# Cutting the first load of a streaming kernel into a 2 KiB head and a 62 KiB body

The kernel runs on one core of one Trainium2 chip. The metric is the device time of that core in microseconds (us), median of several executions. The record calls a kernel slower or faster only from 2% on.

## The reference

```python
x = randn(1024, 4096) float32, axis = -1
mean = np.mean(x, axis=axis, keepdims=True)
out  = ((x - mean) ** 2).astype(np.float32)
```

16.78 MB are read and 16.78 MB written; every row needs all of its 4096 columns before its mean is known.

## The kernel before

Four rows lie side by side in each partition, so 1024 rows make two tiles of 128 partitions x 64 KiB. Each tile is loaded by one DMA and stored by one, and the statistics and squares of a tile are shared between the scalar engine (ACT) and the vector engine (DVE).

```python
x_t = x.rearrange("(n p q) d -> n p (q d)", p=P, q=Q)      # Q = 4 rows a partition
tiles = []
for i in range(ntiles):                                     # ntiles = 2
    x_tile = io.tile([P, Q * D], F32)                       # 64 KiB a partition
    nc.sync.dma_start(out=x_tile, in_=x_t[i])
    tiles.append(x_tile)
# ...
for i in range(ntiles):
    row = [tiles[i][:, q * D:(q + 1) * D] for q in range(Q)]
    m3 = mean_on_act(row[3])
    m0 = mean_on_dve(row[0])
    # ... means of rows 1 and 2, squares in place on ACT and DVE
    nc.sync.dma_start(out=out_t[i], in_=tiles[i])
```

## Time and profile before

| | before |
|---|---|
| time, median of the first 3 runs | 83.25 us (83.16 to 83.27) |
| span in the profile | 81.4 us |
| DMA queue q1 | 96.0% of the span, 576 packets, 33.55 MB |
| DVE, ACT busy | 41%, 43% |

How to read it: the busy shares are of the whole span. A DMA packet here is one run of one partition, so its size is the run length, and each of the 16 DMA engines moves 8 packets of each 64 KiB transfer. After its data each transfer has one 4-byte packet an engine that bumps the semaphore. The lines that carry this are in the prediction below.

### The profile page before, as it was taken

The numbers are of one execution on the slowest core, as the hardware profiler recorded it, in microseconds if no ns is written. First come the engines' busy times: TensorE is split into PE (matmuls) and PEld (weight loads), VectorE is DVE, ScalarE is ACT, GpSimd is POOL, SyncE is SP. The second block draws the span as 40 slices with busy tenths as digits, with TensorE's granted clock in tenths as the row PEclk, the third lists the DMA queues.
The fourth block names the chain that finished last, engine by engine and source line by source line (L and its number), as shares of the span: only waits on it lengthen the run. The fifth ranks groups of instructions, "written<-read, shape, count | busy, mean of one in ns | idle before, by whom it ended". The sixth has DMA issues, their size and how long they took to land.

```text
span 81.4 us, 79 instructions
## 1 busy us (share of the span) xinstructions
DVE 33.4 (41%) x16; ACT 34.7 (43%) x13; POOL 0.2 (0%) x4
## 2 busy tenths in 40 slices
DVE  0000000000089999999439999999900000000000
ACT  6000000000089999999339999999800000000000
POOL 0000000000000000000000000000000000000000
DMA  9099956999982999992999992999997499998390
GB/s 483 32 515 515 483 258 290 515 515 515 515 386 129 515 515 515 515 451 129 451 515 515 515 483 129 418 515 515 515 515 322 193 515 515 515 515 386 161 483 0
DMA packets 577, 33.55 MB, mean 412 GB/s; under 512 B 65, under 2 KB 65, under 8 KB 65
## 3 DMA queue, kind: packets, MB, share of 16 engines
q1 hardware_dynamic: 576, 33.55, 96.0%
q14 instruction: 1, 0.00, 0.0%
HBM read 16.78 MB, written 16.78 MB: 412 GB/s over the span
## 4 chain that ended last, share of the span: by engine, by line
DMA 50%; DVE 21%; SPq 0%; issue 0%
DMA x_tile<-in_x_dram 50%; DVE neg_sum L62 16%; DVE x_tile L85 2%; DVE x_tile L84 1%; DVE neg_mean L65 1%; SPq L46 0%
## 5 line engine op out<-in xcount | busy, mean ns | idle before, releaser
L62 DVE TENSOR_REDUCE neg_sum<-x_tile 128x1 f32<-128x4096 f32 x6 | 26.5, 4413 | 25.2 <-DMA x_tile<-in_x_dram 25.2
L69 ACT ACTIVATE x_tile<-x_tile,neg_mean 128x4096 f32<-128x4096 f32 (+1 forms) x8 | 26.0, 3323 | 0.1
L54 ACT ACTIVATE copy<-x_tile 128x4096 f32<-128x4096 f32 x2 | 7.2, 3617 | 23.3 <-DMA x_tile<-in_x_dram 23.3
L85 DVE TENSOR_TENSOR x_tile<-x_tile 128x1792 f32<-128x1792 f32 x2 | 4.1, 2026 | 0.1
L84 DVE TENSOR_SCALAR x_tile<-x_tile,neg_mean 128x1792 f32<-128x1792 f32 x2 | 2.3, 1154 | 0.1
L54 ACT ACT_TABLE_LOAD x1 | 1.3, 1283 | 0.7 <-PEq L103 0.7
L65 DVE TENSOR_SCALAR neg_mean<-neg_sum 128x1 f32<-128x1 f32 x6 | 0.9, 154 | 0.2
L54 ACT ACTIVATION_READ_ACCUMULATOR copy<-x_tile 128x1 f32 x2 | 0.4, 187 | 0.0
L103 POOL MEMSET const-bfloat16-1.0<- 128x1 bf16 x1 | 0.1, 101 | 0.0
L103 POOL MEMSET const-uint8-127<- 128x1 uint8 x1 | 0.1, 101 | 0.0
L103 POOL MEMSET const-float32-0.0<- 128x1 f32 x1 | 0.1, 98 | 0.2 <-issue 0.2
L103 POOL MEMSET const-float32-1.0<- 128x1 f32 x1 | 0.1, 98 | 0.0
## 6 DMA issues: line engine op xcount, KB each, us to landing
x_tile<-in_x_dram SPq DMA_DIRECT2D x2, 31.4
out_dram<-x_tile SPq DMA_DIRECT2D x2, 21.7
```

The lines of the kernel that those rows point to most:

```text
L54: nc.scalar.activation(out=copy, in_=row, func=ACT.Identity, scale=-inv_d, accum_out=neg_mean)
L62: inorder(nc.vector.reduce_sum(out=neg_sum, in_=row, axis=mybir.AxisListType.X, negate=True))
L65: inorder(nc.vector.tensor_scalar_mul(out=neg_mean, in0=neg_sum, scalar1=inv_d))
L69: inorder(nc.scalar.activation(out=part, in_=part, func=ACT.Square, bias=neg_mean, scale=1.0))
L84: nc.vector.tensor_scalar_add(out=back, in0=back, scalar1=m2)
L85: nc.vector.tensor_mul(out=back, in0=back, in1=back)
L103: nc = _bacc.Bacc("TRN2", target_bir_lowering=False, num_devices=1)
```

## The change

Its intent: let the first transfer begin with a short one. Load 0 becomes a head of 512 columns (2 KiB a partition) and a body of the rest (62 KiB). Load 1 and both stores keep their 64 KiB runs.

```diff
+    HEAD = 512
...
-        nc.sync.dma_start(out=x_tile, in_=x_t[i])
+        cuts = [0, HEAD, Q * D] if i == 0 else [0, Q * D]
+        for lo, hi in zip(cuts, cuts[1:]):
+            nc.sync.dma_start(out=x_tile[:, lo:hi], in_=x_t[i][:, lo:hi])
```

## The prediction

> **What bounds the kernel now.** I read the page first, then the chain of waits, then the timeline, then a table of stretches cut at the four transfers, and last the records of the single DMA packets in the trace. The page's top lines:
>
> ```profile
> DVE 33.4 (41%) x16; ACT 34.7 (43%) x13; POOL 0.2 (0%) x4
> ...
> DMA  9099956999982999992999992999997499998390
> ...
> DMA packets 577, 33.55 MB, mean 412 GB/s; under 512 B 65, under 2 KB 65, under 8 KB 65
> ...
> q1 hardware_dynamic: 576, 33.55, 96.0%
> ```
>
> No compute engine is busy for half the span, while one DMA queue is busy for 96% of it. The dips in the tenths (0, 2, 3) are no idle time: a packet is booked in the slice where it starts, and a packet of 64 KiB lasts 2.4 us, longer than the 2.0 us slice. The 576 packets are 4 transfers x 128 partitions = 512 data packets of 64 KiB, and 4 x 16 = 64 semaphore packets (4 B, 9 ns each).
>
> The chain of waits alone would mislead. It gives DMA 50% and DVE 21% and stops at 58.9 us, at the last vector instruction, in front of the final store. The table of stretches (start:end, us, DVE, ACT, POOL, clock, DMA share, GB/s), cut by me at the transfers, corrects that:
>
> ```profile
> 0.00:1.70 1.70, 0.00 (x0) 0.97 (x1) 0.20 (x4) 1.00 0.00 0
> 1.70:21.60 19.90, 0.00 (x0) 0.31 (x1) 0.00 (x0) 1.00 1.01 422
> 21.60:40.98 19.38, 16.71 (x8) 16.72 (x6) 0.00 (x0) 1.00 1.00 433
> 40.98:60.40 19.42, 16.71 (x8) 16.72 (x6) 0.00 (x0) 1.00 1.00 432
> 60.40:80.30 19.90, 0.00 (x0) 0.00 (x0) 0.00 (x0) 1.00 0.97 422
> 80.30:81.40 1.10, 0.00 (x0) 0.00 (x0) 0.00 (x0) 1.00 0.00 0
> ```
>
> Load, load, store, store follow one another without a pause; the DMA share is 1.00 in the middle, and all compute (16.7 us a tile) lies beside transfers of 19.4 us. So the time is: start until packets move, 32 packets per engine in a row (4 transfers x 128 / 16), and a tail. From the timeline, the two places where the queue could run dry:
>
> ```profile
> 0.73 0.86 SPq L46 DMA_DIRECT2D x_tile<-in_x_dram  x2
> ...
> 39.68 0.35 SPq L86 DMA_DIRECT2D out_dram<-x_tile  x1
> 42.05 3.62 ACT L54 ACTIVATE copy<-x_tile 128x4096 f32<-128x4096 f32 x1 [2.59 <-DMA x_tile<-in_x_dram]
> ```
>
> The packet records give the rest, in us from the span's start. The first packets start at 1.75 (one engine at 2.30), 1.02 after the issue at 0.73. That first round of 16 packets takes 2.72 to 3.41 us each (mean 3.10), ending between 4.74 and 5.44; every later load packet takes 2.42. The spread of 0.70 us between the first and the last engine stays until load 1 is done (40.99 to 41.67) and is still 0.54 at the end (79.77 to 80.31). The last landing follows at 80.65, the span ends at 81.4. The program's end is thus set by the engine that came last out of round one: 5.44 + 31 x 2.415 = 80.31. The quoted time of 83.25 lies 1.8 above the span; I carry that over.
>
> **What the Trainium skill says.** "DMA: Bandwidth & Descriptors", section "Where 436 GB/s comes from", puts the ceiling at 435.2 GB/s, 16 ports x 32 B x 850 MHz. The trace agrees: 433 GB/s in a whole stretch, and 65,536 B in 2.418 us is 27.1 GB/s an engine. No size of run can raise that. Section "Why small descriptors are slow" of that page gives about 3 cycles a packet, 3.5 ns at 850 MHz; no 2 KiB packet is in the trace of before, but 2,418 ns against 65,536 / 27.2 = 2,409 leaves at most 9 ns a packet. Section "Latency and other measured facts" puts the HWDGE first byte at about 600 ns. Here 1.02 us pass from the issue's start to the first packet, 0.64 from its end, and the first packet carries at least 0.57 us over a steady one where it started early. "Perfetto Trace Analysis", section "DMA Optimizations", says that splitting may let chunks start sooner if DMA engines are generally idle. They are not idle here, save for the first 1.75 us, which are before any packet.
>
> **The change, part by part.**
> 1. One more DMA issue on the sync queue. One took 0.38 and the next began at 1.16, so load 0's body is issued at 1.16 and load 1 at about 1.59, which has until 21.6 to be ready. On the path: nothing.
> 2. Bytes stay. Each engine swaps 8 packets of 64 KiB for 8 of 2 KiB and 8 of 62 KiB, and gets one more semaphore packet. At 3.5 to 9 ns for each of 8 packets, plus 9, that is 0.04 to 0.08 us, all on the path as the queue is full. Estimate: +0.06.
> 3. The seam between head and body. The head keeps an engine busy for 16 KiB / 27.1 = 0.60 us. The body's descriptors come 0.43 after the head's (the issue distance). So the body is queued about 0.2 us before the head is drained: no hole if reads run ahead of writes, as they do between the steady packets, which follow without a gap. Estimate: 0.
> 4. The first round. It costs 0.68 us an engine over a steady one (3.10 - 2.42), and 0.44 lies between the mean end (5.00) and the last (5.44). Read latency remains whatever the first packet's size. But the stagger of the engines will be drawn anew: shorter first packets can even it out, up to -0.4, or widen it. I see no reason that it shrinks for certain. Estimate: -0.1.
> 5. Compute. Row 0 spans columns 0 to 4095 and the head holds only 512, so no instruction can start on the head. All wait for the body, and the first compute stays near 22.7. On the path: nothing.
>
> Sum: +0 + 0.06 + 0 - 0.1 + 0 = -0.04, so 83.2.
>
> **The rivals.**
> - The small head gets the engines through the cold start sooner or more evenly. For: the first round is the one place with slack, 0.3 to 1.0 us of excess by engine. Against: the excess looks like the time to the first byte, which a short packet pays too. If all engines ended with the mean: 83.25 - 0.44 + 0.06 = 82.9. If most of the 0.70 spread and part of the latency went: 82.5.
> - The 2 KiB packets are bound by latency and not by bytes. For: the runtime's own 8 KiB instruction fetches took 531 ns where 8,192 / 27.1 = 302 would do, 0.23 more; 8 in a row would add 1.8 us, giving 85.1. Against: those are lone packets, and data packets behind one another hide the latency. Half hidden in part: 83.7 or so.
> - Store 0 comes too late and the queue runs dry. It is issued at 39.68, its first packet starts at 41.14, 1.46 later, while load 1's engines end between 40.99 and 41.67. So the earliest engine already waits 0.15, and the last has 0.53 in hand. For: this margin is thinner than the landing at 42.05 suggests. Against: landing of load 0 and end of load 1 both move with the same packets, so the margin stays; an extra semaphore wait ahead of row 0 costs tens of ns. Even 0.3 us lost here would be hidden from the last engine.
>
> **Range and chances.** The certain costs are under 0.1 us, the redrawing of the stagger is worth -0.4 to +0.4, and runs of before differ by 0.11. That makes 82.7 to 83.8 for 8 in 10, with a little more room above for head packets that hide latency badly. Two per cent are 1.67 us. A gain that large exceeds the whole spread plus the mean latency of round one (0.70 + 0.68 = 1.38), so I give it 2%. A loss that large needs nearly all 8 small packets in series: 4%. Within 2%: 94%.
>
> **What would show each step.** Packets should be 720 (640 data, 80 semaphore), with the same 33.55 MB. The three load issues should start near 0.73, 1.16 and 1.59. The 62 KiB packets should take about 2.34 us, the later 2 KiB ones of a head near 80 ns; 200 ns or more each would show the latency rival. The first compute should start at 22.2 to 23.1 and the two tiles' starts stay 19.34 apart. If the stagger was redrawn, it shows as a change in where the last engine begins its second transfer (22.35 before), and the whole difference in time should already be there. A hole at 41 or 60 us would show the third rival. The prediction is wrong if the stretches in the middle drop below 430 GB/s, or if 62 KiB packets move fewer bytes per ns than 64 KiB ones.

## The result, and the profile after

| | before | after |
|---|---|---|
| median, 6 runs each, same rounds | 83.23 us (83.16 to 83.27) | 83.15 us (82.95 to 83.26) |
| ratio | | 0.999, 95% interval 0.9976 to 1.0003 |

A ratio here is the mean time of one kernel's runs over that of the other's of the same rounds, so it is not quite the ratio of the medians quoted. The two repeats of the change in later batches gave 83.12 against 83.17 (0.9994) and 83.11 against 83.09 (1.0000).

First the page of the changed kernel, its DMA lines (tenths by slice, packets, queue):

```profile
DMA  1999569999974999990999990999992899997490
...
DMA packets 720, 33.55 MB, mean 413 GB/s; under 512 B 80, under 2 KB 80, under 8 KB 208
...
q1 hardware_dynamic: 720, 33.55, 96.2%
```

There are 144 packets more, which is 128 of 2 KiB and 16 semaphore packets. The bytes are the same and so is the queue's share. The table of stretches of the changed kernel, with the same cuts and columns as in the prediction (start:end, us, DVE, ACT, POOL, clock, DMA share, GB/s):

```profile
1.70:21.60 19.90, 0.00 (x0) 0.31 (x1) 0.00 (x0) 1.00 1.00 422
21.60:40.98 19.38, 16.71 (x8) 16.72 (x6) 0.00 (x0) 1.00 1.00 433
40.98:60.40 19.42, 16.71 (x8) 16.72 (x6) 0.00 (x0) 1.00 1.00 435
60.40:80.30 19.90, 0.00 (x0) 0.00 (x0) 0.00 (x0) 1.00 0.97 418
```

Every stretch moves what it moved before, to within 4 GB/s (a packet counts where it starts, so a cut can shift a few). Last, its timeline:

```profile
0.73 1.33 SPq L50 DMA_DIRECT2D x_tile<-in_x_dram  x3
22.39 3.62 ACT L58 ACTIVATE copy<-x_tile 128x4096 f32<-128x4096 f32 x1 [20.38 <-DMA x_tile<-in_x_dram]
22.47 4.42 DVE L66 TENSOR_REDUCE neg_sum<-x_tile 128x1 f32<-128x4096 f32 x1 [22.47 <-DMA x_tile<-in_x_dram]
...
39.42 19.62 SPq L90 DMA_DIRECT2D out_dram<-x_tile  x2
```

The compute starts 0.3 us earlier than before (22.71) in this run, and so does store 0 (39.68). DVE starts 0.08 after ACT. Row 0 now depends on two transfers and row 3 on one, which may be the reason; it is not shown (in the run body_act below row 0 also depends on two, and both engines start at 23.45). This run took 82.95 us, the fastest of the six, so a part of its lead is luck. The packet records tell how much.

**How the packet records were read.** For each transfer I took the start of its first packet on every engine and the start of its semaphore packet, which follows the last data at once. Means over the 16 engines need no knowledge of which packet was on which engine, as long as the first packets can be told from the second ones. In the middle of a transfer the packets follow one another every 80 ns (2 KiB), 2,339 ns (62 KiB) and 2,414 ns (64 KiB). That is a line of 4.7 ns a packet plus 27.2 GB/s an engine. "Lost" is a transfer's length over what this line gives.

In a 2 KiB head the first packets can't be told for certain: the engines start over half a microsecond apart (1.75 to 2.30 in the kernel before), so the 16 earliest starts include second packets (one starts at 1.845, 4 ns before the end of one that ran from 1.768 to 1.849, the overlap that packets in a row show). For heads the table therefore gives two figures, the first from the 16 earliest starts, the second an estimate from chains of packets that follow one another with that overlap. The ends of load 0 don't depend on this. All in us:

| profile | time of that run | first packet, mean start | lost in head | lost in body (with the pause ahead of it) | end of load 0, mean | its last engine | spread, first to last |
|---|---|---|---|---|---|---|---|
| before | 83.21 | 1.908 | - | 0.692 | 21.909 | 22.342 | 0.70 |
| before, again | 83.43 | 1.919 | - | 0.727 | 21.955 | 22.541 | 0.85 |
| after | 82.95 | 1.850 or 1.945 | 0.42 or 0.33 | 0.290 | 21.908 | 22.042 | 0.29 |
| after, again | 83.08 | 1.837 or 1.938 | 0.35 or 0.25 | 0.388 | 21.932 | 22.167 | 0.47 |
| after, third | 83.08 | 1.824 or 1.922 | 0.39 or 0.29 | 0.346 | 21.908 | 22.165 | 0.53 |

Two things stand in it. The mean end of load 0 is the same to 0.05 us in all five profiles. And the time of each run is its last engine's end of load 0 plus 60.87 to 60.92, so what differs between these runs is almost wholly how far the engines are spread at that point.

### The profile page after: what moved, and what is told of

Read it like the earlier page. It is cut to its first block, busy times and chain, and to the rows that moved or that the text cites. A ratio compares the mean times of both kernels' runs of the same rounds, so it can differ in the third digit from the quotient of the medians.

```text
span 81.2 us, 83 instructions
## 1 busy us (share of the span) xinstructions
DVE 33.4 (41%) x16; ACT 34.7 (43%) x13; POOL 0.2 (0%) x4
## 4 chain that ended last, share of the span: by engine, by line
DMA 49%; DVE 21%; SPq 1%; issue 0%
DMA x_tile<-in_x_dram 49%; DVE neg_sum L66 16%; DVE x_tile L89 2%; DVE x_tile L88 1%; SPq L50 1%; DVE neg_mean L69 1%
## 5 line engine op out<-in xcount | busy, mean ns | idle before, releaser
L58 ACT ACT_TABLE_LOAD x1 | 1.3, 1283 | 0.7 <-PEq L107 0.7
```

Of the source, the lines that this page charges most:

```text
L58: nc.scalar.activation(out=copy, in_=row, func=ACT.Identity, scale=-inv_d, accum_out=neg_mean)
```

## The experiments

The theory at this point (A): extra packets cost a few ns each, and the change's only gain is a more even cold start. The rivals: the change does nothing beyond noise (B); the spread is drawn anew in each execution (C); small packets or late issues lose time (L, S). Diffs are against the changed kernel.

### The same packets in the other order: tail2k and swap

```diff
-        cuts = [0, HEAD, Q * D] if i == 0 else [0, Q * D]
+        cuts = [0, Q * D - HEAD, Q * D] if i == 0 else [0, Q * D]
```

> Same packets as the change in the other order: load 0 is first 62 KiB, then 2 KiB a partition. Theory A (each extra packet costs about 9 ns on the path, and the gain of the change is a more even cold start thanks to short first packets): the cost stays and the gain goes, so +0.08 us over before, 83.3 us, with the engines' spread after load 0 near 0.7 us as before. Rival B (the change does nothing but noise, packets and order included): 83.2 us, like before. Rival C (the cold start is drawn anew in each execution, whatever the first packet): 83.15 to 83.3, spread after load 0 anywhere from 0.3 to 0.7 us.

Measured: 83.48 us against 83.23, ratio 1.0031 (1.001 to 1.0053). That is more than the packets' cost, and the timeline shows why:

```profile
22.67 1.28 ACT L58 ACT_TABLE_LOAD   x1 [22.67 <-DMA x_tile<-in_x_dram]
23.97 3.62 ACT L58 ACTIVATE copy<-x_tile 128x4096 f32<-128x4096 f32 x1
...
40.75 0.35 SPq L90 DMA_DIRECT2D out_dram<-x_tile  x1
```

The scalar engine's first instruction now waits for two transfers. One of the waits stands ahead of its table load, which ran at 0.73 to 2.01 us before and now runs after the data has landed. (The load's length of 1.28 us is what the Trainium skill gives, in "ScalarE: Activation LUTs", section "What ACT_TABLE_LOAD costs": about 1,283 ns.) Store 0 goes out at 40.75. The engines end load 1 at 41.12 to 41.51 and start the store at 41.59 to 41.74, a pause of 0.34 us on average. Load 0 itself ended at 21.990 on average, 0.08 after before. So the run is confounded, and I made it again with the small piece cut from row 0:

```diff
-        for lo, hi in zip(cuts, cuts[1:]):
+        for lo, hi in reversed(list(zip(cuts, cuts[1:]))):
```

> The same two DMAs as the change, same columns, issued in the other order: the 62 KiB body first, the 2 KiB piece of row 0 second. Unlike the piece at the row's end, the scalar engine's first instruction waits for one transfer alone, so its table load should stay at 0.7 us and store 0 in time. Theory A (packet cost 0.08 us, gain from the short first packets only): +0.08 us over before, 83.3 us, no pause at 41 us, cold start as before (0.7 us an engine). If the pause at 41 us is there again, or the time is 83.45 or more, the cost of the small packets is larger than 8.7 ns each.

Measured: 83.43 against 83.17, ratio 1.0028 (1.0012 to 1.0044). The table load is back at 0.73 us. Load 0 ends at 22.000 on average, 0.09 over before (expected 0.08), and loses 0.71, as before does. (Against the second profile of before, 21.955, it is 0.045; so the cost is 0.05 to 0.09, and this run can't tell 4.7 ns a packet from 8.7.) The rest comes later. Its store 0 pauses for 0.17 us on average, 0.16 on the last engine, and then takes 19.41 us instead of the 19.31 of the changed kernel, although it was issued at 39.76. So the packet cost is small at load 0, as expected, and +0.26 overall is mostly a store effect that I had not expected (below).

### How much a 2 KiB transfer costs: heads8 and blocks2

```diff
+        cuts = list(range(0, 8 * HEAD, HEAD)) + [8 * HEAD, Q * D] if i == 0 else [0, Q * D]
```

> Eight heads of 2 KiB a partition, one after the other, then a body of 48 KiB: 7 x 8 = 56 more packets an engine than the change, and 7 more semaphore packets. Theory A: 56 x 8.7 ns + 7 x 9 ns = 0.49 to 0.55 us on the path, so 83.65 to 83.7 us, and the spread as in the change. Rival B (packets cost nothing at this size): 83.15 us. Rival L (2 KiB packets wait for latency, or the issue distance of 0.43 us against 0.67 us of data leaves holes): over 84 us.

Measured: 85.15 against 83.23, ratio 1.0227 (1.0205 to 1.0249), slower. Theory A's 0.5 fails and the rival L holds, but it named two causes. The next run keeps the 64 small packets an engine and takes away six of the eight transfers:

```diff
+        cuts = [8 * HEAD, Q * D] if i == 0 else [0, Q * D]
+        if i == 0:
+            blocks = [t[:, : 8 * HEAD].rearrange("p (b two f) -> p b two f", two=2, f=HEAD)
+                      for t in (x_tile, x_t[i])]
+            for half in range(2):
+                nc.sync.dma_start(out=blocks[0][:, :, half], in_=blocks[1][:, :, half])
```

> The same 64 packets of 2 KiB an engine as the eight heads, from the same columns, but in two DMAs of 32 packets (even blocks, odd blocks) and not in eight of 8. If the loss of the eight heads (1.92 us over before, of which the packets' own 8.7 ns explain 0.5) lies at the seams between DMAs, about 0.2 us a seam, then 83.23 + 0.5 + 0.3 = about 84.0 us. If 2 KiB packets lose time by themselves wherever they stand, 85.1 us as the eight heads. If they run clean, 83.7 us.

Measured: 83.83 against 83.17, ratio 1.0077 (1.0062 to 1.0092). That is 0.17 under the seam figure and 0.13 over the clean one. The stretch in which both kernels move nothing but 2 KiB packets, eight heads first, then the two transfers of alternate blocks:

```profile
1.70:7.30 5.60, 0.00 (x0) 0.30 (x1) 0.00 (x0) 1.00 0.90 288
```
```profile
1.70:7.30 5.60, 0.00 (x0) 0.31 (x1) 0.00 (x0) 1.00 0.97 347
```

The last column is GB/s: the same packets move at 288 in transfers of 8 an engine and at 347 in transfers of 32. In the packet records, load 0 ends at 23.51 us on average with eight heads and at 22.26 with alternate blocks; less the 64 packets x 4.7 ns = 0.30, the latter is within 0.05 us of the kernel before. The difference of 1.24 over six further transfers is about 0.2 us each, and the medians say the same (1.92 - 0.66 = 1.26 over before). So 2 KiB packets behind one another run clean (80 ns), and transfers of only eight of them an engine, one after another, do not. Why they lose time is open: the trace has their issues 0.43 to 0.48 us apart, while a head holds 0.64 us of data, so late issues alone don't explain it. My figure of 0.5 us for 56 packets was also too large: 8.7 ns is what the records' durations give, but the records overlap by 4 ns, and the spacing gives 4.7, so 0.26. Of the alternate-block kernel's 0.66, the packets are 0.30; in its profiled run most of the rest goes with a wide spread, 0.94 us at the end of load 0.

### The size of the head: head512b, head8k, head16k

```diff
-    HEAD = 512
+    HEAD = 128      # head512b; 2048 in head8k, 4096 in head16k
```

> Head of 512 B a partition instead of 2 KiB: 8 packets of about 27 ns, 0.22 us an engine, while the body's packets come 0.43 us after the head's. If the seam matters (step 3 of the prediction), an engine is dry for 0.2 us: 83.35 us. If the cold start covers the seam (the first body packets in the change still took 0.0 to 0.5 us over their steady 2.34 us), no loss: 83.1 to 83.2 us.

> Head of 8 KiB a partition: 8 packets of 0.31 us, 2.5 us an engine, so the body is queued 2 us before the head is drained and no seam is possible. If the seam costs the change anything, this one is faster than the change by that much, 82.9 to 83.0 us; if not, it is the same as the change, 83.1 to 83.2 us, with no excess left in the first body packet and the whole excess in the head packets.

> Head of 16 KiB a partition. The 8 KiB head took the cold start's excess from 0.68 to 0.44 us an engine and was 0.2 us faster than before. If any split with no seam risk does that, 83.0 us again. If the excess grows with the first packet's size (8 KiB 0.44, 64 KiB 0.68), 0.5 us and 83.05 us. If the 8 KiB result was luck of the draw, 83.2 to 83.3 us.

| head | this, before (medians) | ratio | lost in head | lost in body, with the pause ahead | end of load 0, mean |
|---|---|---|---|---|---|
| 512 B | 83.64, 83.23 | 1.0046 (1.0026 to 1.0065) | 0.16 or 0.02 | 1.06 | 22.340 |
| 2 KiB (three profiles) | as above | 0.999, 0.9994, 1.0000 | 0.35 to 0.42, or 0.25 to 0.33 | 0.29 to 0.39 | 21.91 to 21.93 |
| 8 KiB | 83.02, 83.23 | 0.9972 (0.9954 to 0.9990) | 0.46 or 0.43 | 0.01 | 21.759 |
| 16 KiB | 83.03, 83.17 | 0.9983 (0.9967 to 0.9999) | 0.65 | 0.00 | 21.884 |

The 512 B head loses more than either expectation said. Its packets run clean at about 26 ns and end at 2.13 on average, then the engines pause for 0.28, and the body still pays the whole cold start (0.77). The time, +0.41, is close to the issue distance of 0.43. So in this run the cold start was not a matter of the first packet: it came with the first stretch of bulk reading, and a head too short to cover the issue distance only delayed it. From 8 KiB on next to nothing is lost at the body (0.00 and 0.01 here, 0.11 in the repeat below).

### Is the 8 KiB head better, and how firm is the spread? after_again, after_third, head8k_again, before_again

The first two are the changed kernel as it stands, the fourth is the kernel before, and the third is the 8 KiB head again; none has a diff of its own.

> The changed kernel itself once more, beside the others on one chip. If the change is a small true gain: 83.0 to 83.15 us with all runs under the median of before. If it was the luck of the draw in the cold start: 83.2 us, overlapping before, and a first round in this profile with another spread than 0.48 us at the first body packets' end.

> The change a third time, to compare with the 8 KiB head on the same chip: 83.1 us, cold loss of the head 0.35 to 0.42 us, body loss 0.28 to 0.35 us, mean end of load 0 at 21.9, spread 0.3 to 0.5 us.

> The head of 8 KiB once more, beside the change on one chip. If its gain is real: 83.0 us, 0.1 under the change and 0.2 under before, with a body loss under 0.05 us and a cold loss near 0.46 us. If it was luck: 83.1 us and a cold loss near 0.65 as with the 16 KiB head.

> The kernel before once more, for a second profile. If the spread of the engines at the end of load 0 (0.70 us) is a property of starting with 64 KiB packets, it is 0.6 to 0.8 again, and the mean end near 21.9. If it is drawn anew each time: anything from 0.3 to 0.8, with the time following the last engine.

Measured: the change 83.12 against 83.17 (82.99 to 83.41, so not all runs lie under the median of before), and 83.11 against 83.09. The 8 KiB head gave 83.30 against 83.09 on this chip, ratio 1.0018 (1.0004 to 1.0032): it is now the slower one. Load 0 was again early (mean 21.737, lost 0.35 + 0.11), but load 1 took 19.57 us an engine where 19.32 is usual. On the first chip it had 19.33. I can't say why. A gain that turns over from chip to chip is none to recommend, so no version here beats both kernels reliably; the 16 KiB head was measured on one chip only.

The kernel before had a spread of 0.85 in its second profile and 83.43 us, while nine other runs of it in that batch took 83.05 to 83.31. So the size of the spread is not a fixed property of starting with 64 KiB packets, which is for rival C; the two profiles stand on different batches, so that it is drawn anew in each execution is likely and not shown. Both profiles of before show a wider spread than all three of the change, but by the rule above (last engine + 60.9, an estimate: the two profiles of the 8 KiB head have 61.1 and 61.4) the median runs of before, 83.09 to 83.23, must have had their last engine near 22.2 to 22.3, where those of the change (83.11 to 83.15) had theirs. Whether the head narrows the spread at all stays open; if it does, by under 0.1 us in the medians.

### The body issued at once with the head: body_act

```diff
-            nc.sync.dma_start(out=x_tile[:, lo:hi], in_=x_t[i][:, lo:hi])
+            queue = nc.sync if hi == HEAD else nc.scalar
+            queue.dma_start(out=x_tile[:, lo:hi], in_=x_t[i][:, lo:hi])
```

> The head stays on the sync queue, while the body and load 1 are issued from the scalar engine's queue, so the body is issued at about 0.73 us together with the head and no longer 0.43 us after it. In the change the body's 8 packets take 0.28 to 0.35 us an engine longer than steady ones. Theory S (that loss is the body coming too late, the issue distance): it goes, mean end of load 0 from 21.91 to about 21.6, time 82.85 to 82.95 us. Rival (the loss is the rest of a cold start of about 0.7 us an engine, due whatever is read first): mean end stays 21.85 to 21.95, time 83.1 to 83.2 us.

Measured: 84.22 against 83.09, ratio 1.0134 (1.012 to 1.0149), slower than either theory allowed. The page's list of transfers of this kernel (issuing queue, KB, us to landing) and its timeline:

```profile
x_tile<-in_x_dram ACTq DMA_DIRECT2D x1, 7936.0 KB, 22.7
x_tile<-in_x_dram SPq DMA_DIRECT2D x1, 256.0 KB, 18.0
```
```profile
0.72 0.88 ACTq L51 DMA_DIRECT2D x_tile<-in_x_dram  x2
0.73 0.37 SPq L51 DMA_DIRECT2D x_tile<-in_x_dram  x1
```

The head of 256 KB lands 18 us after its issue (2.7 in the change): once the body's packets were there, the engines took one 2 KiB packet and one 62 KiB packet in turn. The Trainium skill says so in "DMA: Bandwidth & Descriptors", section "Queues, rings and completion order": an engine goes round the queues it has work for, packet by packet. Here the trace agrees that they take turns; a turn was a single run, where the page has about 9 to 17 descriptors as typical of a packet. The spread at the end of load 0 grew to 1.37 us, and its mean end was 22.154. The run was meant to take the issue distance away, and did not: issued at 0.72 and 0.73, the head's first packet starts at 1.73 and the body's at 2.15, still 0.42 apart (1.72 and 2.21 with the 512 B head, issued 0.43 apart). So it tests neither theory S nor its rival.

### The pause before store 0

A pause between load 1 and store 0, averaged over the engines, shows in some profiles and not in others: 0.09 and 0.19 us in the two of before, 0.17 in the swapped order, 0.19 with the body on the other queue, 0.07 in the first 8 KiB run, and 0.01 in all three of the change. It isn't simply a late issue: with eight heads the store was issued 1.03 us before the first engine ended load 1 and the pause was 0.02, with the swapped order it was 1.29 and they paused. One thing goes with it. Call the time from the store's issue to the first engine's end of load 1 the store's lead. In the five profiles where it was 1.44 us or more (the three of the change, the 16 KiB head, the second of the 8 KiB head) the pause was 0.006 us, the usual seam; in the nine where it was 1.36 or less it was 0.02 to 0.34. The store waits for the last engine's load 0 and the lead is counted to the first engine's end of load 1, so a wide spread shortens it: 0.70 and 0.85 left 1.30 and 1.12 us in the kernel before, 0.29 to 0.53 left 1.65 to 1.44 in the change. The pause's size doesn't follow the lead. In the kernel before it never reached the last engine (in both profiles the latest start of the store lies 5 ns after the latest end of load 1, 41.668 to 41.673 and 41.860 to 41.865), so it costs that kernel nothing; in the swapped order it did. What makes the pause long or short stays open.

## Why the prediction was right

The prediction of 83.2 (82.7 to 83.8, "within 2%") held at 83.15. Step by step:

1. **The extra issue.** Expected at 0.73, 1.16 and 1.59; measured 0.73, 1.16 and 1.64. Nothing of it is on the path. Right.
2. **Packet cost.** Expected +0.06. The spacings give 8 x (80 + 2,339) - 8 x 2,414 = 40 ns an engine. Right, at the low end of what was stated; the 80 ns foreseen for a 2 KiB packet is what the spacing gives (the records last 84). The lower figure used there, 3.5 ns a packet, is an estimate that left a part out (see the closing list); measured are 4.7.
3. **The seam.** Expected 0. The body loses 0.29 to 0.39 us an engine in the three profiles, so the statement "no hole" does not hold as it stands. But the head loses only 0.25 to 0.42, and the two together, 0.62 to 0.74, are about what the single load lost before, 0.69 and 0.73; the mean end of load 0 did not move. So the cold start was shared out, not added to. With a head of 512 B, which can't cover the issue distance, the time rose by 0.41 us, so the working of this step (0.60 us of data against 0.43 us) names a condition that matters. Whether reads run ahead of writes, the condition it named, no run here tests.
4. **The first round.** Expected -0.1 by a redrawn stagger, with up to 0.4 either way. The profiled runs show -0.2 to -0.5 at the last engine (22.04 to 22.17 after, 22.34 and 22.54 before), the medians -0.08, -0.05 and +0.02. The size is inside what was stated, and its sign in the medians is not shown; the -0.1 had no working behind it, so that the first median lay 0.08 lower is luck. That the latency "remains whatever the first packet's size" held for the load as a whole and not for the first packet: part of it moved to the body. That the whole difference of a run should stand at the end of load 0 proved true to 0.05 us.
5. **Compute.** Expected unmoved, first start 22.2 to 23.1, tiles 19.34 apart; measured 22.39 and 41.74, 19.35 apart. Right.

Of the rivals, "latency binds the small packets" fell for packets in a long row (the alternate blocks) and only repeated short transfers lost time, about 0.2 us each, for a reason that stays open; the change has only one. "Store 0 comes too late" rested on a reading that the runs don't bear out: I took the 1.46 us from issue to first store packet as the time that a store needs. In the confounded run the first packets came 0.84 after the issue, so the last engine may have had 41.67 - 39.68 - 0.84 = 1.15 us in hand, not 0.53 (an estimate). That some engines pause when the lead is short (1.36 us or less, near that rival's 1.46), fits all profiles; that it costs the kernel before nothing, as the prediction said, fits too.

## What to carry to other kernels

Where a DMA queue is full from the first packet to the last, as here, the 2 KiB head left the mean end of the first load where it was and moved at most the spread of the engines, and the last engine decided. The 8 KiB head brought that mean end forward by about 0.15 to 0.2 us both times, but the end of the program in one batch of two. Here a head had to hold more time of data than the distance between two issues and stand on the same queue as its body; where it failed either, it cost more than it could bring (0.41 and 1.13 us, one kernel each). More short transfers one after another cost about 0.2 us each. Before you believe a gain of 0.2%, repeat it on another chip and look where in the trace it stands.

## What the Trainium skill lacked or had wrong

- "DMA: Bandwidth & Descriptors" has no figure for the cold start of a bulk load: the 16 engines lost 0.69 and 0.73 us each on average on the first load of the kernel before and at most 0.03 on its second, and the loss was not bound to the first packet (0.77 in the body after a clean 512 B head).
- The same page, "Why small descriptors are slow", gives about 3 cycles a packet and, beside it, 32 B of descriptor metadata for each operation. The prediction used the first alone, 3.5 ns at the 850 MHz of the page's ceiling; the two together, taken as 4 beats of 32 B, are 4.7 ns by my estimate, which is what the spacings of 2 KiB and 64 KiB packets give. So here the page is not wrong. What it has no figure for is short transfers queued one after another: eight DMAs of eight 2 KiB packets an engine lost about 0.2 us for each beyond two, two of 32 lost no more than the cold start.
- "Perfetto Trace Analysis", section "DMA Optimizations", advises splitting where DMA engines are generally idle. It gives no lower bound: a first piece of about 0.2 us, shorter than the issue distance of 0.43 us, cost 0.41; and outlasting it is not enough for many pieces (0.64 us each, eight of them cost 1.92 in all).
- No page that I read has a size for the spread of the engines: before and after, they left the first load 0.3 to 0.9 us apart, were not level again by the end (0.54 in the first profile of before), and the last of them set the time.
- "ScalarE: Activation LUTs", section "What ACT_TABLE_LOAD costs", has the 1.28 us right (1.28 here), but not that the load can end up behind a data wait when the first activation waits for two transfers (22.67 us instead of 0.73), which put the store about 1 us later, 40.75 against 39.76 in the swapped order.
